# A fused DiT block on one core: 2 MB pieces for the last expert weights, transposes in place of matmuls, loads and evictions moved

## The chip, the cores and the metric

One core of one Trainium2 chip runs the whole block. The metric is device time in microseconds (us); the kernel before took 1190.56 us, the median of three runs (1188.13 to 1192.37). All data are float32 unless named otherwise.

## The reference, cut to what matters

A DiT block over 256 tokens of width 1024 with 256 context tokens: modulation vectors from a condition, an input projection, two attention branches of 8 heads each (global, and a window with a sink), gates, an output projection, a router, and 32 experts of which each token uses 4; then a final RMS norm.

```python
h = modulate(rms_norm(x, norm1_g[l]), sh1, sc1)
p = h @ w_in[l]                                   # k, v, q and two gates
y_a = global_attn(q_a, ...); y_b = window_attn(q_b, ..., sink[l])
x = x + g1 * merge_branches(y_a, y_b, g_a, g_b, w_br_a[l], w_br_b[l], w_o[l])
h2 = modulate(rms_norm(x, norm2_g[l]), sh2, sc2)
...
top_logit, top_idx = lax.top_k(t @ w_router + b_router, TOP_K)
for e in range(N_EXPERTS):
    u = t @ w_e1[e] + b_e1[e]                     # 1024 -> 2048
    act = u_glu * sigmoid(SWIGLU_ALPHA * u_glu) * (u_lin + 1)
    out = out + combine[:, e:e + 1] * (act @ w_e2[e] + b_e2[e])
x = x + g2 * out
return rms_norm(x, final_g)
```

Almost all bytes are expert weights: 32 times 8 MB for the first matrix and 4 MB for the second.

## The kernel before, in words

**Weights.** The list `pieces` (lines 45 to 86) names every weight transfer in the order in which it is used; `pump` (line 99) issues them on SP's queue in that order, each into a free part of a ring: four tiles of 8192 columns (4 MB each, `ring`), and later `xxp` (8192 columns, given at line 638) and `r_qt` (4096 columns, given at line 820). `done` (line 141) gives a part back when the matmuls that read it have been written in the program, and calls `pump`; on the chip the issue waits on SP until those matmuls have run. An expert's first matrix is four quarters of 2 MB (two of the eight k-blocks each), its second two halves of 2 MB; experts below `N_ONE = 10` are fetched in these 2 MB pieces. From expert 10 on two neighbouring pieces are one transfer of 4 MB. Expert 31's first matrix is three pieces of 2 MB and two of 1 MB, and the second matrices of experts 30 and 31 come together in column groups (`w2l`): three pieces of 2 MB, two of 1 MB.

**Attention.** Eight units `u` (a pair of heads each), two query halves `qt`. The loop at line 611 holds for each half: two `turn`s (line 549: four transposes of the weights P each into bank `tp`, evicted by ACT for the even and DVE for the odd one), `scores` of the next unit (line 514: two matmuls, DVE maximum over 1024 columns, two Exp on ACT), `y_steps`, once per unit `weigh` of the unit before (line 563: its result goes into the one bank `y`), half a gate projection, the reciprocal of the sums (`norm_p`) and one or two products of the modulation matrix (`mod_v` on DVE, `mod_p` and `mod_a` on POOL and ACT). `y_steps` (line 581) empties the bank `y`: ACT copies its right half (line 578), DVE multiplies (line 579). The order of these calls is the order of the instructions on each engine; nothing reorders them.

**Router.** The loop at line 749 makes the second residual; `stats` and `squares` fill the router's logits. `x1_back` (line 789) then puts the residual, transposed by matmuls with the identity (line 794), into the four accumulator banks `acc`, eight blocks of 128 by 128 for each token half; half 0 stands ahead of the top-k's counts (lines 814 to 818), half 1 behind them. ACT issues the loads of `g2` (a row broadcast to 128 partitions) and `be2` behind the loop (lines 780 and 784). `pick` (line 826) writes the selection matrix that `gather` (line 847) multiplies with.

**Experts.** For each expert e the loop at line 1002 writes: `scatter` of the pair before, bias, `gemm1` (line 881) of the next expert for the k-blocks of its first piece, with the transposes of e's activation (`act_turn`) behind the first k-block, then `gemm2` (line 929) of e, the rest of `gemm1`, and the activation. `steps` (line 982) hangs `spread` and `pick` into an even next expert and `gather` into an odd one, behind a named k-block.

**End.** Five column groups of the last pair (`last2`, line 1041), each with its `share` of the sum, squares and gain; then `total` and `finish` for each token half, and the two output transfers.

Of the kernel before, what the change touches and what calls it, by code (L numbers as in the profile page):

```python
# [18 lines left out]
N_ONE = 10  # L19
# [16 lines left out]
def tile_dit_block(ctx: ExitStack, tc: tile.TileContext, xcT, consts, small, rows,  # L36
# [16 lines left out]
    def w1s(e, ks):  # L53
        if ks in ((0, 1), (2, 3)) and e >= N_ONE:
            pieces.append(("w1", (e, ks[0]), w1[e, ks[0] // 2]))
        else:
            pieces.extend(("w1", (e, k), w1[e, k // 2, :, 4096 * (k % 2):4096 * (k % 2) + 4096]) for k in ks)

    def w2s(e):
        if e < N_ONE:  # L60
            pieces.extend(("w2", (e, k), w2[e, :, 4096 * k:4096 * k + 4096]) for k in range(2))
        else:
            pieces.append(("w2", (e, 0), w2[e]))
# [13 lines left out]
    for e in range(NE - 2):  # L77
        n = 2 if e + 1 >= N_ONE else 1
        w1s(e + 1, tuple(range(n)))
        w2s(e)  # L80
        w1s(e + 1, tuple(range(n, 4)))
# [529 lines left out]
    for u in range(8):  # L611
        for qt in range(2):
            turn(u, 2 * qt)
# [3 lines left out]
            y_steps()  # L617
# [113 lines left out]
    LOW_R, MID_R, ALL_R = slice(96, 128), slice(64, 96), slice(64, 128)  # L731
    for r in (slice(0, 32), MID_R, LOW_R):
        nc.scalar.dma_start(out=braw[r, :], in_=b1e)
# [15 lines left out]
    for m in range(8):  # L749
# [17 lines left out]
        bias_parts(m)  # L767
        if m == 1:
# [11 lines left out]
    nc.scalar.dma_start(out=g2, in_=g2_dram[0:1, :].to_broadcast([128, 1024]))  # L780

    x_t, y_t = t8[0].rearrange("p (a c) -> p a c", a=2), [t8[1].rearrange("p (a c) -> p a c", a=2)]
    be2 = y_t[0][:, 1, 0:512]
    nc.scalar.dma_start(out=be2, in_=b2)
# [4 lines left out]
    def x1_back(tb):  # L789

        for h in range(2):
            acc[tb, h] = ps2.tile([128, 512], F32, name="acc", tag=("xg", "sp")[tb], bufs=2)
            for b in range(4):
                nc.tensor.matmul(acc[tb, h][:, 128 * b:128 * b + 128], x1T[:, 4 * h + b, 128 * tb:128 * tb + 128],
                                 ident, start=(b == 0), stop=False, skip_group_check=True)
# [85 lines left out]
    def gemm1(e, u, ks, between=None):  # L881
        p, j = divmod(e, 2)
        for k in ks:
            if e == NE - 1 and k > 5:
                w = take("l1", k - 6)
            else:
                big = ("w1", (e, 2 * (k // 4) if N_ONE <= e < NE - 1 else k // 2))
                o = 2048 * (k % 4 if N_ONE <= e < NE - 1 else k % 2)
# [7 lines left out]
            elif k % (4 if N_ONE <= e < NE - 1 else 2) == (3 if N_ONE <= e < NE - 1 else 1):  # L896
# [32 lines left out]
    def gemm2(e, aT):  # L929
        p, j = divmod(e, 2)  # L930
        y = ps2.tile([128, 512], F32, name="y", tag="y")
        for k in range(8):
            n = 4 if e < N_ONE else 8
# [48 lines left out]
    def steps(e):  # L982
# [11 lines left out]
        if e == 1:  # L994
            return {3: lambda: gather(p + 1), 6: settle}
        return {3: lambda: gather(p + 1)}
# [5 lines left out]
    for e in range(NE - 2):  # L1002
# [4 lines left out]
        n = 4 if N_ONE <= e + 1 < NE - 1 else 2  # L1007
# [98 lines left out]
    square(4, 1, False)  # L1106
    finish(0)
    total(1)
# [185 lines left out]
```

## Time and profile before

| | |
|---|---|
| median of 3 runs | 1190.56 us (1188.13 to 1192.37) |
| the profiled execution's own time | 1187.26 us |
| its span | 1185.5 us |
| busy: PE (TensorE matmul) | 1108.2 us, 93% |
| busy: DVE (VectorE), ACT (ScalarE), POOL (GpSimd) | 324.8, 143.6 and 48.0 us |
| bytes moved | 458.83 MB, mean 387 GB/s |
| chain that ended last | PE 59%, DMA 34%, DVE 4%, ACT 2% |

SP only issues transfers. "Idle before" of an engine is put down to what ended it. Since matmuls overlap, a busy PE is not a PE at its peak; whether PE or the transfers bound a stretch is read from who waits for whom there.

### The profile page before, as it was taken

To read this page: it belongs to the slowest core of one execution; us is meant where nothing else is said; L and a number is where in the kernel's file an instruction comes from. 1 tells how busy PE (TensorE), PEld (TensorE's weight loads), DVE (VectorE), ACT (ScalarE), POOL (GpSimd) and SP (SyncE) were. 2 spreads that over 40 slices of the span, in tenths; PEclk is the share of its full clock that TensorE was granted. 3 is DMA by queue.
4 is the path that set the end of the run, shared out by engine and by line. 5 is a ranking of instruction groups with operands and counts; after the bars stand their busy time and mean duration, and the time that the engine had idled before them with its cause. 6 is when DMAs were issued, how large, how long until landed. Compare 5 with 4: busy or idle time off the path is not lost.

```text
span 1185.5 us, 13010 instructions
## 1 busy us (share of the span) xinstructions
PE 1108.2 (93%) x5610; PEld 528.0 (45%) x5610; DVE 324.8 (27%) x711; ACT 143.6 (12%) x313; POOL 48.0 (4%) x37
## 2 busy tenths in 40 slices
PE   7999999999999999999999998989898989898986
PEld 5888666894334334343333333333333333333224
DVE  3273666343222221221212112121212121212123
ACT  2122554031000000000000000000000000000002
POOL 0232100030000000000000000000000000000001
PEclk9999999999999999999999999999999999999998
DMA  9995643959999999999999999999999999999994
GB/s 377 380 399 206 221 141 143 392 181 398 429 427 429 427 428 428 427 434 431 427 435 430 427 435 431 431 431 427 434 432 428 434 427 434 431 430 432 427 425 177
DMA packets 28735, 458.83 MB, mean 387 GB/s; under 512 B 3609, under 2 KB 4001, under 8 KB 6049
## 3 DMA queue, kind: packets, MB, share of 16 engines
q1 hardware_dynamic: 26928, 454.05, 90.9%
q10 hardware_dynamic: 1744, 3.90, 1.0%
q8 instruction: 46, 0.75, 0.3%
q14 instruction: 17, 0.13, 0.0%
HBM read 456.88 MB, written 1.05 MB: 386 GB/s over the span
## 4 chain that ended last, share of the span: by engine, by line
PE 59%; DMA 34%; DVE 4%; ACT 2%; issue 1%; ACTq 0%; DVEq 0%
DMA ring<-w 27%; PE u L892 24%; PE y L937 8%; DMA xxp<-w 7%; PE mm L395 3%; PE xg L855 3%; PE qa L296 2%; PE acc L953 2%; PE o L753 2%; PE br L599 2%; ACT xxp L537 1%; PE yl L1047 1%; PE kp L385 1%; PE vp L469 1%; PE ta L925 1%; DVE st L527 1%
## 5 line engine op out<-in xcount | busy, mean ns | idle before, releaser
L892 PE MATMUL u<-ring,t 128*64 128x512 f32 x1552 | 354.0, 602 | 22.2 <-DMA ring<-w 22.1
L892 PEld LDWEIGHTS u<-ring,t 128*64 128x64 f32 x1552 | 108.2, 138 | 231.6 <-issue 193.7
L937 PE MATMUL y<-ring,tmp 128*64 128x512 f32 x768 | 169.9, 594 | 17.3 <-DMA ring<-w 11.0
L944 DVE TENSOR_TENSOR t<-y,r_kv 64x512 f32<-64x512 f32 x60 | 41.3, 688 | 334.2 <-PE y L937 333.6
L937 PEld LDWEIGHTS y<-ring,tmp 128*64 128x64 f32 x768 | 53.6, 137 | 120.9 <-issue 100.1
L892 PE MATMUL u<-xxp,t 128*64 128x512 f32 x416 | 96.9, 613 | 5.4 <-DMA xxp<-w 5.4
L909 ACT ACTIVATE tmp<-tmp 128x512 f32<-128x512 f32 (+1 forms) x33 | 20.3, 617 | 629.0 <-DVE tmp L908 629.0
L908 DVE TENSOR_SCALAR tmp<-u 128x512 f32<-128x512 f32 (+1 forms) x33 | 22.3, 675 | 227.8 <-PE u L892 215.9
L855 PEld LDWEIGHTS xg<-r_kv,r_y 128*128 128x128 f32 x512 | 58.4, 192 | 12.2 <-issue 12.2
L855 PE MATMUL xg<-r_kv,r_y 128*128 128x128 f32 x512 | 61.3, 278 | 0.0
L395 PE MATMUL mm<-xxp,ring 128*128 128x256 f32 x256 | 59.9, 385 | 0.0
L953 PE MATMUL acc<-t,r_kv 128*128 128x512 f32 x120 | 59.5, 618 | 0.0
L857 DVE TENSOR_TENSOR t<-xg,modb 128x512 f32<-128x512 f32 x32 | 22.1, 691 | 132.9 <-PE xg L855 132.9
L892 PEld LDWEIGHTS u<-xxp,t 128*64 128x64 f32 x416 | 29.3, 140 | 63.5 <-issue 53.0
L395 PEld LDWEIGHTS mm<-xxp,ring 128*128 128x128 f32 x256 | 47.3, 190 | 12.6 <-issue 5.0
L937 PE MATMUL y<-xxp,tmp 128*64 128x512 f32 x176 | 39.0, 594 | 4.7 <-DMA xxp<-w 3.1
L1071 POOL TENSOR_TENSOR ring<-ring 128x256 f32<-128x256 f32 (+1 forms) x8 | 5.1, 660 | 894.4 <-DMA ring<-rows 892.7
L953 PEld LDWEIGHTS acc<-t,r_kv 128*128 128x128 f32 x120 | 20.3, 189 | 38.7 <-issue 38.7
L296 PE MATMUL qa<-xxp,ring 128*128 128x256 f32 x128 | 30.7, 388 | 0.0
L926 ACT COPY tmp<-ta 128x512 f32<-128x512 f32 x30 | 17.6, 585 | 103.5 <-PE ta L925 103.5
L753 PE MATMUL o<-r_qt,ring 128*128 128x256 f32 x128 | 28.9, 380 | 0.0
L353 DVE SCALAR_TENSOR_TENSOR ring<-ring,crow 128x1024 f32<-128x1024 f32 x22 | 26.3, 1211 | 0.0
(237 smaller groups left out, 852.7 us busy)
## 6 DMA issues: line engine op xcount, KB each, us to landing
ring<-w SPq DMA_DIRECT2D x49, 4096.0 KB, 40.4
ring<-w SPq DMA_DIRECT2D x47, 2048.0 KB, 18.5
xxp<-w SPq DMA_DIRECT2D x13, 4096.0 KB, 40.7
xxp<-w SPq DMA_DIRECT2D x10, 2048.0 KB, 16.5
ring<-w_mod SPq DMA_DIRECT2D x16, 1024.0 KB, 10.7
r_qt<-w SPq DMA_DIRECT2D x6, 2048.0 KB, 21.5
ring<-w_in SPq DMA_DIRECT2D x10, 1024.0 KB, 8.5
ring<-w_m SPq DMA_DIRECT2D x8, 1024.0 KB, 12.4
```

What stands on the lines that cost most here:

```text
L296: nc.tensor.matmul(qa[c // 4][:, c % 4, :], w[:, 128 * c:128 * c + 128], x[:, j, :], start=(j == 0 and c % 2 == 0), stop=(j == 7), skip_gr ...
L353: nc.vector.scalar_tensor_tensor(out=w, in0=w, scalar=1.0, in1=crow, op0=ALU.mult, op1=ALU.mult, accum_out=moda[:, t:t + 1])
L395: nc.tensor.matmul(gp[0][:, 0:256], w[:, k, :], x[:, k, :], start=(k == 0), stop=(k == 7))
L599: nc.tensor.matmul(ps[:, 0:256], w[:, k, 128 * (m % 2):128 * (m % 2) + 128], Y[:, 4 * br + k, :], start=(k == 0), stop=(k == 3))
L753: nc.tensor.matmul(ps[:, 0:256], w[:, k, :], M[:, k, :], start=(k == 0), stop=(k == 7))
L855: nc.tensor.matmul(xp[:, b, :], z[:, tb, 128 * k:128 * k + 128], S[:, tb, :], start=(tb == 0), stop=(tb == 1))
L857: nc.vector.tensor_tensor(out=XT[p][:, 4 * h:4 * h + 4, :], in0=xp, in1=sh2[:, 4 * h:4 * h + 4].unsqueeze(2).to_broadcast([128, 4, 128]), ...
L892: nc.tensor.matmul(u[c0:c0 + 64, ch % 2, :], XT[p][:, k, 64 * j:64 * j + 64], w[:, 512 * ch:512 * ch + 512], start=(e == 0 and k == 0), st ...
L908: nc.vector.tensor_scalar(out=w(glu), in0=v[:, bs, 0, :], scalar1=LIMIT, scalar2=None, op0=ALU.min)
L937: nc.tensor.matmul(y[64 * h:64 * h + 64, :], l, w[:, 512 * h:512 * h + 512], start=(k == 0), stop=(k == 7))
L944: nc.vector.tensor_tensor(out=YY[p][64 * j:64 * j + 64, 512 * h:512 * h + 512], in0=y[64 * h:64 * h + 64, :], in1=g2[64 * h:64 * h + 64, 5 ...
L953: nc.tensor.matmul(acc[tb, h], t[:, tb, :], y[:, s], start=False, stop=False, skip_group_check=True)
```

## The change

It does six things. Experts from `N_TWO = 29` on are fetched in 2 MB pieces again (expert 29 and 30's first matrices, expert 29's second), and `gemm1` and `gemm2` follow. `y_steps` moves from behind the next unit's scores to the head of each half. The loads of `g2` and `be2` are issued in the output projection's loop at m = 2, `be2` into another tile. The residual's matmuls with the identity carry `is_transpose`. `gather` hangs behind k-block 2 in place of 3. At the end `total(1)` stands ahead of `finish(0)`.

```diff
@@ -16,7 +16,7 @@
 DRAM = bass.MemoryType.DRAM
 
 NE = 32
-N_ONE = 10
+N_ONE, N_TWO = 10, 29
 CAP = 64
 EPS = 1e-6
 ALPHA = 1.702
@@ -51,13 +51,13 @@
         pieces.extend(("mod", i, w_mod[i]) for i in ids)
 
     def w1s(e, ks):
-        if ks in ((0, 1), (2, 3)) and e >= N_ONE:
+        if ks in ((0, 1), (2, 3)) and N_ONE <= e < N_TWO:
             pieces.append(("w1", (e, ks[0]), w1[e, ks[0] // 2]))
         else:
             pieces.extend(("w1", (e, k), w1[e, k // 2, :, 4096 * (k % 2):4096 * (k % 2) + 4096]) for k in ks)
 
     def w2s(e):
-        if e < N_ONE:
+        if not N_ONE <= e < N_TWO:
             pieces.extend(("w2", (e, k), w2[e, :, 4096 * k:4096 * k + 4096]) for k in range(2))
         else:
             pieces.append(("w2", (e, 0), w2[e]))
@@ -75,7 +75,7 @@
     pieces.extend(("wo", i, w_o[i]) for i in range(4))
     w1s(0, range(4))
     for e in range(NE - 2):
-        n = 2 if e + 1 >= N_ONE else 1
+        n = 2 if N_ONE <= e + 1 < N_TWO else 1
         w1s(e + 1, tuple(range(n)))
         w2s(e)
         w1s(e + 1, tuple(range(n, 4)))
@@ -610,11 +610,12 @@
 
     for u in range(8):
         for qt in range(2):
+
+            y_steps()
             turn(u, 2 * qt)
             turn(u, 2 * qt + 1)
             if u < 7:
                 scores(u + 1, qt)
-            y_steps()
             if u and qt == 0:
                 weigh(u - 1)
             if u < 7:
@@ -729,6 +730,7 @@
     braw = t8[1]
     b1e = b1.rearrange("(e c) n -> e (c n)", c=4)
     LOW_R, MID_R, ALL_R = slice(96, 128), slice(64, 96), slice(64, 128)
+    be2 = msc[:, 1:3, :].rearrange("p a b -> p (a b)")
     for r in (slice(0, 32), MID_R, LOW_R):
         nc.scalar.dma_start(out=braw[r, :], in_=b1e)
 
@@ -765,6 +767,10 @@
             stats(*pend)
         pend = (m, zt)
         bias_parts(m)
+        if m == 2:
+            nc.scalar.dma_start(out=g2, in_=g2_dram[0:1, :].to_broadcast([128, 1024]))
+
+            nc.scalar.dma_start(out=be2, in_=b2)
         if m == 1:
 
             ws = mtx[:, 3, :].rearrange("p (k e) -> p k e", k=8)
@@ -777,11 +783,7 @@
             nc.vector.tensor_tensor(out=lb, in0=lp[:, 0:32], in1=brb, op=ALU.add)
     squares(sqs)
     stats(*pend)
-    nc.scalar.dma_start(out=g2, in_=g2_dram[0:1, :].to_broadcast([128, 1024]))
-
     x_t, y_t = t8[0].rearrange("p (a c) -> p a c", a=2), [t8[1].rearrange("p (a c) -> p a c", a=2)]
-    be2 = y_t[0][:, 1, 0:512]
-    nc.scalar.dma_start(out=be2, in_=b2)
 
     nc.scalar.activation(out=junk, in_=eps, func=AF.Exp)
     acc = {}
@@ -792,7 +794,7 @@
             acc[tb, h] = ps2.tile([128, 512], F32, name="acc", tag=("xg", "sp")[tb], bufs=2)
             for b in range(4):
                 nc.tensor.matmul(acc[tb, h][:, 128 * b:128 * b + 128], x1T[:, 4 * h + b, 128 * tb:128 * tb + 128],
-                                 ident, start=(b == 0), stop=False, skip_group_check=True)
+                                 ident, start=(b == 0), stop=False, is_transpose=True, skip_group_check=True)
 
     x1_back(0)
     nc.vector.reciprocal(rt, rt)
@@ -884,8 +886,8 @@
             if e == NE - 1 and k > 5:
                 w = take("l1", k - 6)
             else:
-                big = ("w1", (e, 2 * (k // 4) if N_ONE <= e < NE - 1 else k // 2))
-                o = 2048 * (k % 4 if N_ONE <= e < NE - 1 else k % 2)
+                big = ("w1", (e, 2 * (k // 4) if N_ONE <= e < N_TWO else k // 2))
+                o = 2048 * (k % 4 if N_ONE <= e < N_TWO else k % 2)
                 w = take(*big)[:, o:o + 2048]
             for ch in (0, 2, 1, 3):
                 c0 = 64 * (ch // 2)
@@ -893,7 +895,7 @@
                                  w[:, 512 * ch:512 * ch + 512], start=(e == 0 and k == 0), stop=(e > 0 and k == 7))
             if e == NE - 1 and k > 5:
                 done("l1", k - 6)
-            elif k % (4 if N_ONE <= e < NE - 1 else 2) == (3 if N_ONE <= e < NE - 1 else 1):
+            elif k % (4 if N_ONE <= e < N_TWO else 2) == (3 if N_ONE <= e < N_TWO else 1):
                 done(*big)
             if between and k in between:
                 between[k]()
@@ -930,7 +932,7 @@
         p, j = divmod(e, 2)
         y = ps2.tile([128, 512], F32, name="y", tag="y")
         for k in range(8):
-            n = 4 if e < N_ONE else 8
+            n = 8 if N_ONE <= e < N_TWO else 4
             w = take("w2", (e, k // n)).rearrange("p (k c) -> p k c", k=n)[:, k % n, :]
             l = aT[:, k % 4, 64 * (k // 4):64 * (k // 4) + 64]
             for h in range(2):
@@ -992,8 +994,8 @@
                 s[5] = lambda: pick(p + 1)
             return s
         if e == 1:
-            return {3: lambda: gather(p + 1), 6: settle}
-        return {3: lambda: gather(p + 1)}
+            return {2: lambda: gather(p + 1), 6: settle}
+        return {2: lambda: gather(p + 1)}
 
     u0 = ps2.tile([128, 2, 512], F32, name="u", tag="u")
     gemm1(0, u0, range(8), steps(0))
@@ -1004,7 +1006,7 @@
         if p:
             scatter(p - 1, (j,))
         u = bias1(e + 1)
-        n = 4 if N_ONE <= e + 1 < NE - 1 else 2
+        n = 4 if N_ONE <= e + 1 < N_TWO else 2
         gemm1(e + 1, u, (0,))
         aT = act_turn(e)
         gemm1(e + 1, u, range(1, n), steps(e + 1))
@@ -1104,8 +1106,8 @@
     total(0)
     square(3, 1, False)
     square(4, 1, False)
+    total(1)
     finish(0)
-    total(1)
     finish(1)
 
 
```

How the change moves instructions at three places follows, as the built programs have them. First DVE in the attention, around the second half of unit 1. L579 is the multiplication that empties bank `y`, L556 the eviction of an odd turn, L527 the maximum of the scores, L547 the reciprocal, L353 a product of the modulation matrix. Before:

```order
L353 SCALAR_TENSOR_TENSOR ring_65,moda<-ring_65,crow 128x1024
L556 COPY xxp<-tp 128x4x128
L527 TENSOR_REDUCE st<-s 128x2
L530 TENSOR_TENSOR st<-st,nrs 128x2
L579 TENSOR_TENSOR r_y<-y,r 128x256
L547 RECIPROCAL st<-st 128x2
```

DVE at the same place of the changed program:

```order
L353 SCALAR_TENSOR_TENSOR ring_65,moda<-ring_65,crow 128x1024
L579 TENSOR_TENSOR r_y<-y,r 128x256
L556 COPY xxp<-tp 128x4x128
L527 TENSOR_REDUCE st<-s 128x2
L530 TENSOR_TENSOR st<-st,nrs 128x2
L547 RECIPROCAL st<-st 128x2
```

The multiplication has moved ahead of the eviction and the maximum; on ACT the copy (L578) has moved ahead of the even eviction in the same way.

Second, SP's queue at the end, from the last 4 MB pieces to the final gains (128x8192 is 4 MB, `ring_62` to `ring_65` are the ring's tiles). Before:

```order
L135 DMA ring_65<-w 128x8192
L135 DMA ring_62<-w 128x8192
L135 DMA xxp<-w 128x8192
L135 DMA ring_63<-w 128x8192
L135 DMA ring_64<-w 128x8192
L135 DMA ring_65<-w 128x8192
L135 DMA r_qt<-w 128x4096
L135 DMA ring_62<-w 128x4096 x2
L135 DMA xxp<-w 128x2048 x2
L135 DMA xxp<-w2l 128x4096
```

SP's queue from the same weight on in the changed program:

```order
L135 DMA r_qt<-w 128x4096
L135 DMA ring_65<-w 128x8192
L135 DMA ring_62<-w 128x4096 x2
L135 DMA xxp<-w 128x4096 x2
L135 DMA ring_63<-w 128x4096 x2
L135 DMA ring_64<-w 128x4096 x2
L135 DMA r_qt<-w 128x4096
L135 DMA ring_65<-w 128x4096 x2
L135 DMA ring_62<-w 128x4096
L135 DMA ring_62<-w 128x2048 x2
L135 DMA xxp<-w2l 128x4096 x2
```

Five transfers of 4 MB have become ten of 2 MB, the first and the last of which go to `r_qt`; the bytes and the order of the weights are the same.

Third, PE where expert 30's first matrix (L892 before, L894 with the change) runs beside expert 29's second (L937, then L939); `ta` is the activation's transposes, `tq` those of the scatter matrix. Before:

```order
L892 MATMUL u<-ring_63,t_70 64x512 x4
L925 MATMUL ta<-keep,tmp_1339 128x128 x4
L892 MATMUL u<-ring_63,t_70 64x512 x12
L875 MATMUL tq<-keep,tmp_1339 128x128 x2
L937 MATMUL y<-ring_64,tmp_1339 64x512 x16
L892 MATMUL u<-ring_65,t_70 64x512 x16
```

PE at the same place of the changed program:

```order
L894 MATMUL u<-xxp,t_70 64x512 x4
L927 MATMUL ta<-keep,tmp_1339 128x128 x4
L894 MATMUL u<-xxp,t_70 64x512 x4
L939 MATMUL y<-ring_63,tmp_1339 64x512 x16
L894 MATMUL u<-ring_64,t_70 64x512 x8
L877 MATMUL tq<-keep,tmp_1339 128x128 x2
L894 MATMUL u<-ring_64,t_70 64x512 x8
L894 MATMUL u<-r_qt,t_70 64x512 x8
```

Two k-blocks stand ahead of the second matrix in place of four, and the last six come from three pieces in place of one.

## Rows read from the trace of the kernel before

**Rows 1.** The page's slices of the span: GB/s moved in each of 40.

```profile
GB/s 377 380 399 206 221 141 143 392 181 398 429 427 429 427 428 428 427 434 431 427 435 430 427 435 431 431 431 427 434 432 428 434 427 434 431 430 432 427 425 177
```

**Rows 2.** PE's waits over the span: for whom, us in total, times, longest.

```profile
PE u L892 <- DMA ring<-w: 22.1, 14, 2.7
...
PE y L937 <- DVE t L857: 7.8, 10, 0.8
...
PE y L569 <- DVE r_y L579: 4.3, 6, 1.7
```

**Rows 3.** Stretches (us): each engine's busy time, then granted clock, DMA share, GB/s.

```profile
278.00:279.00 1.00, 1.00 (x8) 0.32 (x6) 0.00 (x0) 0.00 (x0) 0.00 (x0) 1.00 0.12 49
300.00:500.00 200.00, 198.09 (x958) 75.38 (x955) 45.13 (x89) 9.99 (x18) 0.00 (x0) 1.00 1.01 428
600.00:1100.00 500.00, 457.98 (x2142) 169.88 (x2144) 96.22 (x188) 23.63 (x42) 0.00 (x0) 0.98 1.00 431
603.00:604.00 1.00, 1.00 (x4) 0.24 (x2) 0.00 (x0) 0.00 (x0) 0.00 (x0) 0.50 0.84 360
```

**Rows 4.** SP's timeline, 260 to 292 us: start, length, what is issued.

```profile
271.20 0.33 SPq L135 DMA_DIRECT2D r_qt<-w  x1
278.32 7.20 SPq L135 DMA_DIRECT2D ring<-w  x3
```

**Rows 5.** The page's DMA issues: count, KB each, median us from issue to landing.

```profile
ring<-w SPq DMA_DIRECT2D x49, 4096.0 KB, 40.4
ring<-w SPq DMA_DIRECT2D x47, 2048.0 KB, 18.5
```

**Rows 6.** Timeline of one attention unit: start, us, engine, line; brackets: idle before, releaser.

```profile
168.38 0.69 DVE L556 COPY xxp<-tp 128x512 f32<-128x512 f32 x1
...
173.49 0.69 DVE L556 COPY xxp<-tp 128x512 f32<-128x512 f32 x1
...
175.20 1.04 PE L553 MATMUL tp<-keep,xxp 128*128 128x128 f32 x8
...
177.45 0.43 DVE L579 TENSOR_TENSOR r_y<-y,r 128x256 f32<-128x256 f32 x1 [1.75 <-ACT r L578]
...
177.93 0.66 PE L569 MATMUL y<-keep,st 128*64 128x128 f32 x8 [0.42 <-DVE r_y L579]
...
179.19 0.69 DVE L556 COPY xxp<-tp 128x512 f32<-128x512 f32 x1
```

**Rows 7.** The same timeline, where the last unit begins.

```profile
199.54 0.66 PE L569 MATMUL y<-keep,st 128*64 128x128 f32 x8 [1.69 <-DVE r_y L579]
```

**Rows 8.** Timeline of the router, 266 to 272 us.

```profile
266.94 1.95 PE L794 MATMUL acc<-keep,r_qt 128*128 128x128 f32 x16
...
268.70 0.20 DVE L810 TENSOR_SCALAR mask_b<-r_kv 128x64 bf16<-128x64 f32 x1
...
269.09 2.03 PE L794 MATMUL acc<-keep,r_qt 128*128 128x128 f32 x16
...
269.59 0.98 DVE L831 TENSOR_SCALAR r_kv<-keep,rankm,rt 128x64 f32<-128x64 f32 x4
...
270.96 3.74 PE L855 MATMUL xg<-r_kv,r_y 128*128 128x128 f32 x32
```

**Rows 9.** PE's timeline, the last 70 us.

```profile
1119.13 7.09 PE L937 MATMUL y<-ring,tmp 128*64 128x512 f32 x32 [1.52 <-DMA ring<-w]
1128.89 7.09 PE L892 MATMUL u<-ring,t 128*64 128x512 f32 x32 [2.67 <-DMA ring<-w]
...
1165.03 3.67 PE L1047 MATMUL yl<-ring,t 128*64 128x256 f32 x32
```

**Rows 10.** Timeline of the last 10 us, DVE: second token half's total and reciprocal.

```profile
1178.01 0.15 DVE L1074 TENSOR_REDUCE fin<-fin 128x1 f32<-128x4 f32 x1
...
1178.71 0.16 DVE L1082 RECIPROCAL fin<-fin 128x1 f32<-128x1 f32 x1 [0.36 <-ACT fin L1077]
```

**Rows 11.** The chain that ended last: start, us, what.

```profile
601.24 8.78 PE u L892 x32
```

## The prediction

> **What bounds the kernel now.** I read the page first: its slices of GB/s [rows 1] show two stages. From the eleventh slice on (about 300 us) the rate stands at 425 to 435 in all but the last; ahead of that it rises and falls, down to 141. So from about 280 us to the end the transfers bound the time, and before it something else does. PE's list of waits [rows 2] agrees: what PE waits for most is a weight in the ring, 22.1 us under the first line alone. Next, SP's timeline [rows 4] and a fine cut [rows 3] show what starts the full-rate stage: at 278 to 279 us the transfers run at 49 GB/s, and the issue at 278.32 ends that. That issue waits for PE to have read the first piece of expert 0. All that follows goes at 428 to 431 GB/s whatever PE does. The rule for this kernel: what brings PE earlier at 278 us shifts the whole stream, and with it the end; what brings PE earlier inside the stream only makes it wait longer; and what PE still has to do behind the last weights comes on top.
>
> Ahead of 278 us PE itself is busy nearly all the time. Its only repeated wait in the attention is for bank `y`: 4.3 us in six times, the longest 1.7 [rows 2].
>
> **The attention's eviction first.** The multiplication that frees the bank stands behind the next scores' maximum and exponentials, so PE waits 0.42 us at 177.93 [rows 6] and 1.69 at the last unit [rows 7]. Moved ahead of the turns it finds its input long ready and the bank is free half a unit earlier. All 4.3 us could go: the upper bound. The lower bound is the chain on DVE and ACT. From one odd eviction to the next it takes 5.11 us in the half without the multiplication (168.38 to 173.49) and 5.70 in the half with it (to 179.19) [rows 6]. The half that loses it falls to 5.11; the half that gains it grows by the 0.35 us that DVE gives it before its next instruction. A unit then takes 10.57 in place of 10.81, 0.24 less; over the five full units 1.2 us. Which end? PE would save 2.6 us (4.3 less the 1.69 of the last unit) in these units, the chain 1.2; PE may run ahead of the chain by the time between the odd eviction's end and the transposes that reuse its bank, which start at 175.20, the odd ones 0.5 later [rows 6]: 1.5 us, less 0.35 for the later eviction. 1.2 and 1.15 make 2.35. The last unit's 1.69 goes almost whole, since that eviction now stands a full half earlier: 1.55. I take **3.9 us**, and keep 1.2 and 4.3. What waits behind the moved multiplication, the odd eviction, has that same slack; ACT's copy is covered by its idle time ahead of the exponentials.
>
> **Transposes.** Eight matmuls with the identity take 1.95 us (they run as 16 passes) [rows 8]; eight transposes of the same shape in the attention 1.04 [rows 6]. That is 0.9 for each half. [...] The first half saves nothing: PE then waits for the mask, which DVE ends at 268.90, where PE was through at 268.89 [rows 8]. Behind the second half stands `gather`, which needs the selection written from 269.59 to 270.57; it started at 270.96. So 0.4 is sure and 0.9 the most; I take **0.45**. The matmuls into the same accumulators are not shown as transposes in this trace, so that they gain nothing is the lower bound.
>
> **Early loads.** Two ACT issues and 0.75 MB leave 267 us, where the stream is busy, for some 247, in the slice that moves only 181 GB/s [rows 1]. ACT's work behind them isn't on PE's path, and the stream is idle before 278.32 anyway [rows 3]: **0**. It keeps the issue at 271.20, past which it moves, clear when all comes 4 us earlier.
>
> **`gather` one k-block earlier.** It removes 7.8 us of PE's waits (ten times 0.8 [rows 2]), all in experts where PE waits for the stream afterwards: **0**. It puts 3.8 us of matmuls [rows 8] ahead of a release; a transfer is issued 40.4 us before it lands, at 4 MB [rows 5], of which it moves for 9.7, so 30 us cover that.
>
> **2 MB pieces at the end.** Weights land 9.76 us apart for 4 MB (1119.13 to 1128.89), and PE needs 7.09 for them [rows 9]. At 1128.89 PE starts on 4 MB; with two pieces half of it is read by then, and PE is through 3.55 us earlier. From there on weights land each 4.88 us for 2 MB, 2.44 for 1 MB: 6, 2, then three column groups of 2 MB each, the last of these at 1128.89 + 7 x 4.88 = 1163.05. PE takes it up at 1165.03 [rows 9]; it can be at most **1.95** earlier, and 3.5 of lead, less some 1.2 of waiting for expert 31's third piece, suffice for that. The bounds are 0 and 2.4. Against it, 20 MB more go in 2 MB pieces, which ran at 428 GB/s where 4 MB ran at 431 [rows 3]: 49 us by 0.7%, **0.3 lost** (0 to 0.3). `r_qt`, idle before until the end, takes the first piece, so no place is missing.
>
> **The end.** The second half's total and root take 0.70 us from 1178.01 to 1178.71 [rows 10] behind the first half's scaling; now they run beside it, and cost the first half's output 0.4, which isn't last. DVE's own two short operations stay: **0.35** (0 to 0.4).
>
> **Sum.** 3.9 + 0.45 + 1.95 + 0.35 - 0.3 = 6.35, say 6.3. The profiled execution took 1187.26 us (span 1185.5): 1181.0 with the change. It stands 3.3 below the median of the three runs, 1190.56; for a median I forecast **1184.3**.
>
> **Rivals.**
> [...]
> - *DVE's chain alone sets the attention*: 1.2 in place of 3.9, 1187.0. Against it, the slack above. 0.10.
> - *The front's gain never reaches the stream*, because another wait holds the issue at 278.32: only the tail is left, 1188.6. Against it, transfers are idle just then [rows 3]. 0.10.
> - *The finer end does not do what it says*, PE having other waits there: 1186.2. 0.05.
> - *Slower: the release behind `gather`.* In nine odd experts with 4 MB pieces the release comes 3.8 us later. It decides where less than 3.8 us of issued work is left for the transfers; then up to 9 x 3.8 = 34 us are added, 1218. Against it 40.4 us [rows 5]; for it the first 2 MB pieces, 18.5 us, where cover is thin at one place. 0.03.
>
> **Numbers.** The forecast has 0.60. A measurement of this kernel can tell 0.3% from no change, 3.6 us: faster is below 1187.0. From the cases: 0.60 x 0.95 + 0.12 x 0.85 + 0.10 x 0.5 + 0.10 x 0.15 + 0.05 x 0.85 makes 0.78, with the rest of the cases 0.19 for the same, and 0.03 slower. The range: all upper bounds together give 1.6 less, and three runs spread by 2 to each side, so I start at 1181.0; the upper end takes in the stream that doesn't shift, 1188.6.
>
> **What would show it.** PE's wait for `y` at the weighing gone, and the last weighing at about 206 in place of 209.8; the issue of the first piece after expert 0's at about 274; the second `acc` group of the residual near 1 us; ten waits for the gather's eviction gone, with the waits for the ring longer by as much; no wait over 1.5 us behind the last pieces; granted clock 1.00 through the router. The prediction is wrong if the stream begins no earlier, if PE waits for odd evictions in the attention, or if the rate of the last 50 us falls under 428.

## The result, and the profile after

| | before | after |
|---|---|---|
| median of 6 runs each | 1190.75 us (1188.13 to 1192.37) | 1183.08 us (1180.77 to 1185.55) |
| the profiled execution | 1187.26 us, span 1185.5 | 1182.69 us, span 1180.9 |

The ratio of the times is 0.9945 (95% interval 0.9926 to 0.9963): 0.55% faster. The medians lie 7.7 us apart, the two profiled executions 4.6; where the other 3 us are is told with the experiments.

First the attention. The first and the last weighing in PE's timeline of the kernel before (start, length, instruction):

```profile
134.55 0.66 PE L569 MATMUL y<-keep,st 128*64 128x128 f32 x8
...
209.83 0.66 PE L569 MATMUL y<-keep,st 128*64 128x128 f32 x8
```

The same of the changed kernel, the weighings of units 0, 1, 5, 6 and 7:

```profile
134.67 0.66 PE L569 MATMUL y<-keep,st 128*64 128x128 f32 x8
144.70 0.66 PE L569 MATMUL y<-keep,st 128*64 128x128 f32 x8
...
186.36 0.66 PE L569 MATMUL y<-keep,st 128*64 128x128 f32 x8
195.63 0.66 PE L569 MATMUL y<-keep,st 128*64 128x128 f32 x8
206.28 0.66 PE L569 MATMUL y<-keep,st 128*64 128x128 f32 x8
```

None has a bracket any more: the waits for bank `y` [rows 6, 7] are gone. The first weighing starts 0.12 later than before (134.55), the last at 206.28 in place of 209.83, so from first to last it is 71.61 us where it was 75.28: **3.67 gained**.

Two small waits of PE are new. In the second halves of three units the eight transposes of the turns take 1.25 to 1.27 us in place of 1.04, because the weight load (PEld) waits for the odd eviction, which now stands behind the multiplication. And in the last unit PE waits for ACT's tanh of a gate, which empties bank `mm` (L397):

```profile
173.34 1.25 PE L553 MATMUL tp<-keep,xxp 128*128 128x128 f32 x8
...
173.94 0.42 PEld L553 LDWEIGHTS tp<-keep,xxp 128*128 128x128 f32 x4 [0.23 <-DVE xxp L556]
...
198.30 3.72 PE L599 MATMUL mm<-r_y,ring 128*128 128x256 f32 x16 [0.28 <-ACT t L397]
```

The first three distances between weighings are 10.03 to 10.32 us, the next two 10.53 and 10.56.

The router, the same instructions as in [rows 8]:

```profile
263.39 1.04 PE L796 MATMUL acc<-keep,r_qt 128*128 128x128 f32 x8
265.15 0.20 DVE L812 TENSOR_SCALAR mask_b<-r_kv 128x64 bf16<-128x64 f32 x1
265.40 0.19 PE L816 MATMUL rk<-mask_b,tri 128*128 128x32 bf16 x1 [0.98 <-DVE mask_b L812]
265.54 1.07 PE L796 MATMUL acc<-keep,r_qt 128*128 128x128 f32 x8
266.03 0.98 DVE L833 TENSOR_SCALAR r_kv<-keep,rankm,rt 128x64 f32<-128x64 f32 x4
267.21 3.81 PE L857 MATMUL xg<-r_kv,r_y 128*128 128x128 f32 x32 [0.60 <-PE acc L796]
```

Eight transposes take 1.04 and 1.07 us, where eight matmuls took 1.95 and 2.03. Most of both savings turns into PE's waits: 0.98 for the mask, as forecast, and 0.60 in front of the gather. That second bracket names PE's own residual, which had ended 0.6 before; what ended last is VectorE's selection, 266.03 + 0.98 = 267.01. The gather starts 0.20 behind it, where it was 0.39 [rows 8], and takes 3.81 us in place of 3.74. The first release of the weight stream shows what is left. SP's queue:

```profile
266.69 0.33 SPq L135 DMA_DIRECT2D r_qt<-w  x1
274.65 7.19 SPq L135 DMA_DIRECT2D ring<-w  x3
```

From the last weighing to this issue it is 68.37 us; before it was 278.32 - 209.83 = 68.49 [rows 4, 7]. So transposes, early loads and the earlier issue of the piece in `r_qt` gave **0.12** together.

PE's waits over the span (for whom, total, times, longest), the three that answer to [rows 2]:

```profile
PE u L894 <- DMA ring<-w: 25.7, 20, 2.6
PE y L939 <- DMA ring<-w: 10.6, 7, 1.5
...
PE u L894 <- DMA r_qt<-w: 1.2, 1, 1.2
```

The ten waits of 0.8 for the gather's eviction are gone, and those for the ring are longer in sum. The stream still sets the pace. Stretches of 300 to 500, 600 to 1060 and 1060 to 1160 us (busy time of each engine, granted clock, DMA share, GB/s):

```profile
300.00:500.00 200.00, 198.03 (x958) 75.46 (x957) 45.78 (x89) 10.63 (x19) 0.00 (x0) 1.00 1.01 428
600.00:1060.00 460.00, 422.23 (x1976) 155.11 (x1974) 88.56 (x170) 22.43 (x40) 0.00 (x0) 0.99 1.00 431
1060.00:1160.00 100.00, 93.78 (x458) 35.90 (x456) 20.80 (x44) 7.62 (x15) 0.00 (x0) 0.98 1.00 424
```

PE at the last weights, against [rows 9]:

```profile
1125.48 3.65 PE L894 MATMUL u<-r_qt,t 128*64 128x512 f32 x16 [1.24 <-DMA r_qt<-w]
...
1140.17 7.09 PE L894 MATMUL u<-ring,t 128*64 128x512 f32 x32 [0.97 <-DMA ring<-w]
...
1159.93 3.67 PE L1049 MATMUL yl<-ring,t 128*64 128x256 f32 x32 [0.16 <-DMA ring<-w2l]
```

Expert 30's last weights are there at 1125.48, where they were at 1128.89: 3.41 earlier, so 0.26 of the front's gain is lost on the way; that the slower pieces cost it is borne out by the run with 2 MB pieces alone, below. PE takes up the third column group 34.45 us later in place of 36.14: **1.69** gained. From there to the last copy of a sum it is 10.92 us in both. The end before (VectorE's last copy, the second output's issue; then KB and us from issue to landing):

```profile
1175.95 0.52 DVE L1058 COPY ring<-acc 128x128 f32<-128x128 f32 x2 [0.36 <-PE acc L1057]
...
1179.82 0.35 ACTq L1088 DMA_DIRECT2D out<-ring  x1
```
```profile
out<-ring ACTq DMA_DIRECT2D x1, 512.0 KB, 3.8
```

The end of the changed kernel (with both issues):

```profile
1170.85 0.52 DVE L1060 COPY ring<-acc 128x128 f32<-128x128 f32 x2 [0.36 <-PE acc L1059]
...
1173.31 0.34 SPq L1090 DMA_DIRECT2D out<-ring  x1
...
1174.18 0.35 ACTq L1090 DMA_DIRECT2D out<-ring  x1
```
```profile
out<-ring SPq DMA_DIRECT2D x1, 512.0 KB, 3.1
out<-ring ACTq DMA_DIRECT2D x1, 512.0 KB, 5.3
```

From that copy to the last issue it is 3.33 us in place of 3.87 (1175.95 to 1179.82): 0.54 gained. But the two outputs are issued 0.87 apart, not 1.58, and the second lands 5.3 us after its issue, where before it took 3.8. From the last issue to the end of the execution's time it is 8.51 us, against 7.44: 1.07 given back.

The profiled executions add up: -0.12 + 3.67 + 0.12 - 0.26 + 1.69 + 0.54 - 1.07 = 4.57. The first term (the start, which the change doesn't touch) and the last (the landing) differ from one execution to the next; the five between them make 5.76.

### The profile page after: what moved, and what is told of

It reads as the page before. It is cut to its first block, busy times and chain, and to the rows that moved or that the text cites. A ratio compares the mean times of both kernels' runs of the same rounds, so it can differ in the third digit from the quotient of the medians.

```text
span 1180.9 us, 12994 instructions
## 1 busy us (share of the span) xinstructions
PE 1107.9 (94%) x5594; PEld 526.3 (45%) x5594; DVE 326.5 (28%) x711; ACT 143.4 (12%) x313; POOL 47.4 (4%) x37
## 4 chain that ended last, share of the span: by engine, by line
PE 61%; DMA 36%; DVE 1%; issue 1%; ACT 1%; ACTq 0%; SPq 0%; DVEq 0%
DMA ring<-w 23%; PE u L894 21%; PE y L939 9%; DMA xxp<-w 6%; PE xg L857 5%; PE mm L395 5%; DMA r_qt<-w 3%; DMA ring<-w2l 3%; PE qa L296 2%; PE o L755 2%; PE acc L955 2%; PE br L599 2%; PE s L519 1%; PE kp L385 1%; PE vp L469 1%; PE tp L553 1%
## 5 line engine op out<-in xcount | busy, mean ns | idle before, releaser
L894 PE MATMUL u<-ring,t 128*64 128x512 f32 x1552 | 357.7, 605 | 25.8 <-DMA ring<-w 25.7
L894 PEld LDWEIGHTS u<-ring,t 128*64 128x64 f32 x1552 | 107.2, 139 | 234.8 <-issue 186.9
L939 PE MATMUL y<-ring,tmp 128*64 128x512 f32 x768 | 169.4, 593 | 10.6 <-DMA ring<-w 10.6
L939 PEld LDWEIGHTS y<-ring,tmp 128*64 128x64 f32 x768 | 54.4, 137 | 117.5 <-issue 105.3
L894 PE MATMUL u<-xxp,t 128*64 128x512 f32 x400 | 92.6, 606 | 6.4 <-DMA xxp<-w 6.2
L894 PEld LDWEIGHTS u<-xxp,t 128*64 128x64 f32 x400 | 27.6, 138 | 59.3 <-issue 48.0
L939 PE MATMUL y<-xxp,tmp 128*64 128x512 f32 x176 | 38.9, 593 | 3.0 <-DMA xxp<-w 3.0
L353 DVE SCALAR_TENSOR_TENSOR ring<-ring,crow 128x1024 f32<-128x1024 f32 x22 | 26.3, 1211 | 0.0
```

What stands on the lines that cost most here:

```text
L353: nc.vector.scalar_tensor_tensor(out=w, in0=w, scalar=1.0, in1=crow, op0=ALU.mult, op1=ALU.mult, accum_out=moda[:, t:t + 1])
L894: nc.tensor.matmul(u[c0:c0 + 64, ch % 2, :], XT[p][:, k, 64 * j:64 * j + 64], w[:, 512 * ch:512 * ch + 512], start=(e == 0 and k == 0), st ...
L939: nc.tensor.matmul(y[64 * h:64 * h + 64, :], l, w[:, 512 * h:512 * h + 512], start=(k == 0), stop=(k == 7))
```

## Experiments

The theory, from here on T: the time is start + attention + router + a stream of fixed length + what stands behind its last weights; each edit is worth what it does to its own summand. Rivals stand with each run. The first four ran on one chip beside the kernel before (1188.49 us, median of 23 runs), the next four on another (1190.24, 15 runs), the last four on a third (1191.46, 11 runs). So only ratios or traces are compared across the chips.

**The attention alone, and all but the attention.** In the kernel before `y_steps` goes to the head of the half; in the changed one it goes back.

```diff
+            y_steps()
             turn(u, 2 * qt)
             turn(u, 2 * qt + 1)
             if u < 7:
                 scores(u + 1, qt)
-            y_steps()
```

> The kernel before with only the eviction of bank y moved to the head of each half. My theory (PE ran ahead of the DVE chain, and the front's gain passes to the stream one to one): the last weighing starts near 206.3 us in place of 209.8, the issue behind expert 0's first piece near 274.8 in place of 278.3, and the run is 3.5 us shorter than before (3 to 4). Rival (the DVE and ACT chain alone sets the pace): last weighing near 208.3, 1.2 to 1.7 us shorter. Rival (the stream does not follow the front): the weighing moves, the time stays within 1 us.

> The change without the attention's move. My theory: the last weighing is back at 209.8 us with six waits for bank y, 4.3 us in all; the issue behind expert 0's first piece at 278.1, 0.2 earlier than before; the time is 3.5 us over the changed kernel's and 2 to 4 under the kernel before. Rival (most of the gain lies in the finer pieces at the end): within 1.5 us of the changed kernel.

Alone: 1184.92 us, ratio 0.9970 (0.9957 to 0.9982). Undone: 1186.15, ratio 0.9980 (0.9967 to 0.9992). First to last weighing 71.57 and 75.29 us. So the attention is worth 3.6 to 3.7 in the weighings and 3.57 in the medians, and the rest of the change about 2.3 in the medians: 5.9 in all on this chip, near the 5.76 of the steps. Release behind last weighing: 68.48 and 68.37, the same 0.11 for the transposes. But the profiled execution of the attention alone took 1188.17 us, longer than the kernel before's own. Stretches show why (16 to 19, 21 to 24, 1127.4 to 1136 us):

```profile
16.00:19.00 3.00, 2.07 (x18) 1.79 (x17) 1.71 (x5) 1.17 (x2) 1.65 (x2) 1.00 1.02 415
21.00:24.00 3.00, 3.00 (x15) 2.45 (x12) 0.87 (x3) 0.37 (x1) 0.00 (x0) 0.71 1.05 427
...
1127.40:1136.00 8.60, 8.58 (x32) 2.59 (x32) 0.00 (x0) 0.00 (x0) 0.00 (x0) 0.80 0.99 423
```

Twice the granted clock falls from the 1.00 of the first stretch: to 0.71 and to 0.80. Near 20 us, after waits of 0.68 and 0.25, it moves the first weighing to 136.83, 2.3 later than before. At 1127.42, after a wait of 2.64 us for expert 30's last 4 MB, 32 matmuls take 8.78 us in place of 7.09:

```profile
1127.42 8.78 PE L892 MATMUL u<-ring,t 128*64 128x512 f32 x32 [2.64 <-DMA ring<-w]
```

The kernel before's profiled execution has neither at these two places.

**The pieces undone.** The changed kernel with 4 MB pieces up to expert 30 (expert 31 was finer in both).

```diff
-N_ONE, N_TWO = 10, 29
+N_ONE, N_TWO = 10, 31
```

> The change with the last experts' weights in 4 MB pieces as before. My theory: PE reaches the third column group of the last pair 1.7 us later against the landing of expert 30's last weights (36.1 us behind it in place of 34.4), so 1.7 us over the changed kernel. Rival (2 MB pieces lower the stream's rate and eat it): no difference, the landing of expert 30's last weights 0.3 us or more earlier than in the changed kernel and the tail longer by as much. Rival (most of the median's gain over the profile's is a clock drop in the tail that finer pieces avoid): 3 us or more over, with granted clock under 1 behind 1080 us.

1184.02 us, ratio 0.9959 (0.9944 to 0.9974); the profiled execution took 1188.37 and again has the fall at the start (first weighing 136.64) and in the tail:

```profile
1128.92 8.55 PE L894 MATMUL u<-ring,t 128*64 128x512 f32 x32 [2.64 <-DMA ring<-w]
```

From the first release to the last output's issue: 902.47 us here, 899.53 in the changed kernel, 901.50 in the kernel before, which has the old end order (0.54) and no fall. The pieces without a fall are thus worth 901.50 - 899.53 - 0.54 = 1.43 net, and with it 2.94: the theory's 1.7 (less the rate's 0.26) and the last rival's 3 both occur, in different executions. A third loss shows here, the only other one in front of the release (timeline, 237 to 245 us):

```profile
239.67 2.05 POOL L740 CAST be<-t 32x2048 bf16<-32x2048 f32 x1 [26.32 <-DMA t<-b]
239.89 2.11 DVE L777 TENSOR_TENSOR t<-r_kv,modb 128x256 f32<-128x256 f32 x1
242.04 2.59 DVE L779 TENSOR_TENSOR t<-t 128x128 f32<-128x128 f32 x3
242.12 2.20 POOL L747 TENSOR_TENSOR t<-t,be 64x1024 f32<-64x1024 f32 x1 [0.40 <-ACT be L745]
...
244.68 0.41 PE L782 MATMUL lp<-t,ones 128*128 128x32 f32 x2 [1.45 <-DVE t L779]
```

VectorE's multiplication took 2.11 us, as long as GpSimd's cast beside it lasted (0.42 where it began no later than the cast), and the additions behind it 2.59 beside GpSimd's next instruction (0.78 in the changed kernel's first profile). PE waited 1.45, and the release came 70.09 us after the last weighing.

**The end undone.**

```diff
-    total(1)
     finish(0)
+    total(1)
     finish(1)
```

> The change with the second half's total behind the first half's finish again. My theory: the last output's issue comes 0.4 to 0.5 us later behind the last eviction of the accumulator (3.9 us in place of 3.3), and the time is within 0.5 us of the changed kernel's. Rival (two outputs issued 0.9 us apart in place of 1.6 land later by what was won, 5.3 us in place of 3.8 from issue): the last landing comes at the same distance from the last eviction, so nothing is won.

1182.76 us, ratio 0.9949 (0.9935 to 0.9962), where the changed kernel has 0.9945. Its end:

```profile
1171.16 0.52 DVE L1060 COPY ring<-acc 128x128 f32<-128x128 f32 x2 [0.36 <-PE acc L1059]
...
1173.45 0.34 SPq L1090 DMA_DIRECT2D out<-ring  x1
1175.04 0.35 ACTq L1090 DMA_DIRECT2D out<-ring  x1
```

3.88 us from copy to issue against 3.33: the 0.55 at the issue is real. What it is worth in time is blurred by the landing of the second output. With the new order that took 4.0 to 5.3 us in eleven profiles, with the old one 3.8 to 4.5 in three; from copy to the end of the time that makes 10.5 to 11.8 and 11.3 to 12.0, on average 11.1 and 11.6. The two ranges overlap, so the gain is shown at the issue; in time 0.5 is only the likeliest value, and the rival (nothing won) is not ruled out.

**The transposes undone.** The residual's blocks are turned by plain matmuls again.

```diff
-                                 ident, start=(b == 0), stop=False, is_transpose=True, skip_group_check=True)
+                                 ident, start=(b == 0), stop=False, skip_group_check=True)
```

> The changed kernel with its residual transposes as plain matmuls again. Theory (the faster transposes hardly help, because the gather waits for the router's pick on VectorE, not for the residual): a pass of eight takes 1.95 us instead of 1.04, the router's matmuls for both token blocks come some 0.9 us later each, VectorE's pick still ends within 0.2 us of where it does in the changed kernel relative to the last attention weighing, and the time is 0 to 0.3 us longer. What changes is only when PE reaches the gather. Rival (the prediction's own term): the gather and with it the last release come 0.45 us later, the median is 0.45 us longer. Rival 2: both passes are on the path, +1.8 us.

1181.74 us, ratio 0.9935 (0.9920 to 0.9950): not slower. The release stands 68.49 us behind the last weighing, 0.12 more than with transposes. In the trace the first expectation holds, and 0.45 and 1.8 are out; 0.12 us in the time is less than six runs can tell, and the changed kernel did not run beside this one. The distance is that of the kernel before (68.49), so the early loads, which no run undoes by themselves, are worth nothing in it.

**The gather back.**

```diff
-        return {2: lambda: gather(p + 1)}
+        return {3: lambda: gather(p + 1)}
```

> The changed kernel with the gather of the next pair one step later again (after gemm step 3). Theory (the weights bound that stretch): some ten waits of 0.8 us of PE for VectorE's copy of the gathered tokens come back, 7 to 8 us in all; the waits for weights shrink by as much (25.7 to about 22 us), and the time is the same within 0.3 us. Rival (PE's lost time reaches the end): slower by up to 7 us.

1183.83 us, ratio 0.9951 (0.9933 to 0.9969). PE's list of waits:

```profile
PE u L894 <- DMA ring<-w: 22.2, 19, 2.8
...
PE y L939 <- DVE t L859: 7.1, 9, 0.8
```

The gather's waits are back and the ring's shorter; from the release to the last issue it is 899.56 us against 899.53. The gather's place is worth nothing, as T has it. In front of the release this execution lost time twice: the 1.45 of the cast, and this in the router (the second pass; stretches of 260 to 266.4 and 266.4 to 268.4 us):

```profile
266.46 1.95 PE L796 MATMUL acc<-keep,r_qt 128*128 128x128 f32 x8
```
```profile
260.00:266.40 6.40, 5.41 (x42) 4.83 (x41) 2.45 (x15) 3.27 (x8) 0.48 (x2) 0.97 0.63 223
266.40:268.40 2.00, 2.00 (x14) 1.91 (x15) 1.64 (x8) 1.89 (x4) 0.00 (x0) 0.50 1.01 434
```

The granted clock is 0.50, right behind the wait of 0.98 for the mask. The transposes take 1.95 in place of 1.07, and so use up the wait in front of the gather; the gather, still in part at the lower clock (0.87 from 268.4 to 272.5 us), takes 4.37 in place of 3.81:

```profile
268.20 4.37 PE L857 MATMUL xg<-r_kv,r_y 128*128 128x128 f32 x32
```

The release comes 70.72 us behind the last weighing. Where only the cast got in the way it came 70.1 behind (three profiles, 70.08 to 70.16), so this fall cost 0.6. The next run shows both losses too (70.58 us, the gather 4.34), so there the fall cost 0.5.

**All expert weights in 2 MB pieces.**

```diff
-N_ONE, N_TWO = 10, 29
+N_ONE, N_TWO = 10, 10
```

> The changed kernel with every expert's weights in 2 MB pieces (no 4 MB pieces at all). Theory (rate): the stretch from 300 to 1060 us flows at about 428 GB/s instead of 431, so some 0.7% of 760 us: 4 to 5 us slower, and the last landing is later by as much. Rival 1 (the rate of the last stretch was low for another reason): same rate, same time within 0.5 us. Rival 2 (clock): the long waits of TensorE for 4 MB pieces become short ones, the granted clock of the stretch rises from 0.97 to 1.00, but as the weights bound it, that alone changes nothing in the time.

1186.17 us, ratio 0.9970 (0.9958 to 0.9982). The stretch:

```profile
600.00:1060.00 460.00, 416.51 (x1962) 151.44 (x1960) 87.65 (x166) 22.09 (x39) 0.00 (x0) 1.00 1.01 428
```

The rate is 428, not 431, and from the release to the last issue it is 903.90 us, 4.37 more: the rate's price, as expected. The granted clock is 1.00 (PE's longest wait for a piece in the ring is 1.3 us, where it was 2.6), and PE is busy 416.5 us where it was 422.2, with no gain. For each of the 19 experts from 10 to 28 the finer pieces cost 0.23 us; so the 20 MB of experts 29 and 30 cost about 0.4 (an estimate from this run), and 2 MB pieces pay only where PE's last work hangs on them.

**The last unit alone.**

```diff
+            if u > 5:
+                y_steps()
             turn(u, 2 * qt)
...
+            if u < 6:
+                y_steps()
             if u and qt == 0:
```

> The changed kernel with a unit's result leaving its bank at the old place for units 0 to 5 and at the new one for the last units only. Theory (each unit's wait of PE for the bank is worth its own 0.4 to 0.7 us, and the last one 1.2 to 1.7 us): from the first to the last weighing 73.3 to 73.7 us, between the 75.29 of the old place and the 71.61 of the new one; the granted clock does not matter here. Rival (the first units' waits are absorbed by VectorE's chain anyway, and only the last wait counts): 71.6 to 72.2. Rival 2 (the last one counts nothing): 75.0 to 75.3.

PE's first and last weighing (one execution):

```profile
134.12 0.66 PE L569 MATMUL y<-keep,st 128*64 128x128 f32 x8
...
207.67 0.66 PE L569 MATMUL y<-keep,st 128*64 128x128 f32 x8
```

First to last weighing 73.55 us, in place of 75.28 and 71.61. The last wait is worth 1.73 of the 3.67, the five before it 1.94 together. Both parts of the sum are there.

**Three losses that come and go.** Edits against two of them: `fill(n)` writes n matmuls of 128x128 into an unread part of a bank, in PE's waits at the start; the cast goes from GpSimd to ScalarE, three steps later (with the transposes' edit of above).

```diff
     crow_half(0)
+    fill(4)
     crow_half(1)
+    fill(1)
...
             m0_turn(k // 2)
+            if k == 0:
+                fill(2)
...
         if m == 0:
-            nc.gpsimd.tensor_copy(be1[0:32, :], braw[0:32, :])
+            return
+        if m == 3:
+            nc.scalar.copy(out=be1[0:32, :], in_=braw[0:32, :])
```

> The changed kernel as it is, once more, beside the three that follow. Theory (three small losses come and go from one execution to the next: TensorE at half its granted clock near 20 us, at half in the second pass of transposes in the router, and VectorE slowed beside the cast on GpSimd near 240 us; 2.0, about 2 and 1.45 us each): its times spread over some 4 to 5 us with the median near 1183, and its profile shows any of the three or none. Rival (the spread is the rate of the transfers): the stretch from 600 to 1060 us moves at another rate than 431 GB/s in the slower ones.

> The changed kernel with seven matmuls of 128x128 into an unread part of a bank, put into TensorE's short waits between 16 and 19 us. Theory (the waits there let the clock fall): the granted clock stays 1.00 from 0 to 25 us in this profile, the median is 0.5 to 1 us below the changed kernel's, since the fall was seen in 2 of 8 profiles so far and costs 2 us. Rival (the fall has another cause): it comes as often, and the matmuls themselves cost 0 to 0.5 us.

> The changed kernel with the residual transposes as plain matmuls again, and the cast of the first biases from GpSimd to ScalarE, three steps later. Theory (both are losses that come and go): no granted clock under 1.00 from 260 to 276 us, no wait of TensorE over 0.3 us for VectorE near 244 us, last release 68.3 to 68.5 us behind the last weighing, and a median 1.0 to 2.0 us below the changed kernel's. Rival 1 (the transposes are as good as the matmuls, their fall of the clock was chance): the same median as with the cast alone, 0.5 us below. Rival 2 (the cast on ScalarE holds up its squares): slower by up to 1 us.

> All three edits: the matmuls in the waits at the start, the plain matmuls instead of the transposes, the cast on ScalarE. Theory: the times lie closer together (within 2 to 3 us) and the median is 1.5 to 2.5 us below the changed kernel's, near 1180.5 to 1181.5, faster than both kernels. Rival: no better than the better of its two parts.

| | median (lowest to highest) | ratio to before |
|---|---|---|
| the changed kernel again | 1181.83 (1180.77 to 1183.56) | 0.9931 (0.9912 to 0.9949) |
| start filled | 1181.87 (1181.45 to 1183.97) | 0.9929 (0.9911 to 0.9946) |
| matmuls, cast on ScalarE | 1181.60 (1181.31 to 1184.03) | 0.9928 (0.9909 to 0.9946) |
| all three | 1182.61 (1181.82 to 1182.72) | 0.9933 (0.9915 to 0.9950) |

None is faster than the changed kernel: the expected 0.5 to 2.5 us are a miss, and so is the changed kernel's expected spread of 4 to 5 us: it is 2.8. With all three the six times lie within 0.9 us where the others spread over 2.5 to 2.8, so in six runs it took away spread and no median. The rival on the rate is out: the stretch from 600 to 1060 us moves at 431 GB/s in every profile but that of the run with 2 MB pieces alone. Neither filled profile has the fall near 20 us, but it is in only two of the twelve others, so whether the fill prevents it is not shown. What the fill costs isn't either: first weighings at 135.40 and 134.79, where the unfilled profiles without the fall have 133.82 to 135.00. In the two profiles with the cast on ScalarE PE does not wait at 240 us, and the release is 68.48 behind the last weighing; the start-filled one had the cast in its way (1.53, 70.16). The profile of the changed kernel run again had none of the losses, at 1180.77 us:

```profile
273.98 0.33 SPq L135 DMA_DIRECT2D ring<-w  x1
```
```profile
out<-ring ACTq DMA_DIRECT2D x1, 512.0 KB, 4.0
```

Beside the kernel before's profiled execution, 1187.26, that is 6.49 us: start 0.48, attention 3.74, router 0.12, slower stream -0.32, tail 1.68, end 0.54, and 0.25 behind the last issue. Without the start and the landing it is 5.76 again.

## Why the prediction was right

It said 1184.3 us (1181.0 to 1188.6), faster with 0.78; the median was 1183.08. Its likeliest case is the one that came. Its sum of 6.3 us was made for like executions; two executions without any of these losses lie 6.49 apart, but 0.73 of that is start and landing, and the steps themselves make 5.76. So the nearness of 6.3 and 6.49 is in part luck, and so is that of the median, which had 7.7 to fall and started from a median with losses in it (last point).

| step | forecast | measured |
|---|---|---|
| attention's eviction | 3.9 | 3.67 and 3.74 (3.57 in medians) |
| transposes | 0.45 | 0.12 |
| early loads, gather | 0 | 0 in the traces |
| 2 MB pieces | 1.95 | 1.69 and 1.68 |
| the slower rate | -0.3 | -0.26 and -0.32 |
| the end's order | 0.35 | 0.54 at the issue; in time some 0.5, not clear of the landing |

- *Attention.* The price lies between the chain's 1.2 and PE's waits, as the sum had it. The part for five units was forecast at 2.35 (1.2 of the chain and 1.15 of slack) and the last one's at 1.55; the run with the last unit alone gives 1.94 and 1.73. PE runs ahead of the chain for three units and then goes at its pace: 10.53 and 10.56 us a unit, where the forecast had the chain at 10.57. PE's waits of 0.2 for the odd evictions are that chain. The prediction's list of signs counts such a wait as being wrong, which its own sum does not bear out. What the sum lacks is the wait of 0.28 in the last unit for ACT's tanh; it is absent where only the last unit moves, and is likely most of the 0.4 by which the five units came out too high.
- *Transposes* is the step that was mis-sized. "0.4 is sure" took the gather to stand 0.4 behind the selection because of PE. In the changed kernel it starts 0.20 behind the selection's end even with PE idle for 0.60, and takes 0.07 longer; the selection itself comes no earlier (60.73 us behind the last weighing, before 60.74), since VectorE's chain makes it. The 0.9 that each pass saves is real and worth 0.12.
- *Pieces.* 7 pieces of 2 MB were to take 4.88 us each; the 34.45 us between make it 4.92. That is 0.29 over the seven, enough for the difference of 0.26. Another sign of being wrong, a rate under 428 in the last 50 us, was badly chosen: from 1110 to 1160 us the kernel before had 424 already, and the changed one has 422.
- *Rivals.* The front's gain did reach the stream (the release 3.67 earlier, the landings 3.41), the finer end did what it says, and nowhere did the gather hold up a release: 899.53 and 899.56 us. The 0.12 in the sum of chances is for a fall of the clock in the router. No run shows that number; what the runs showed is the fall in two of nine profiles with transposes (the second eight at 1.95 us in place of 1.07, the granted clock 0.50 in the one above), and in none of five with plain matmuls. Whether it lies with the transposes is not settled, since seven profiles with them have no fall, and plain matmuls also fill PE's wait of 0.98 for the mask. In both profiles with the fall the cast had got in PE's way too, so the two may hang together; that was not tried. It cost 0.6 and 0.5 us, less than the 1.7 by which 32 matmuls in the stream grew (8.78 us [rows 11] in place of 7.09 [rows 9]), since the second pass's loss fell into PE's wait of 0.60 in front of the gather.
- *The median.* What the forecast missed is that the median of before holds a loss that its profile doesn't have. Of three profiles with 4 MB pieces at the end two show the fall of the clock behind the wait of 2.64 us, 1.5 to 1.7 us each; of eleven with 2 MB pieces, where PE's waits for a piece are 1.34 at most, none does. So the pieces are worth 1.4 us in an execution without the fall and some 3 in one with it. The same fall comes all through the stream, and there no cost shows, since PE waits less for the next pieces: in the kernel before's profile 0.83 us for weights between the 8.78 at 601.24 and the next wait of 2.62, but 2.23 between the 7.09 at 718.89 and the next wait of 2.62. The changed kernel's own profile has one behind its last long wait, for expert 28:

```profile
1066.82 8.57 PE L894 MATMUL u<-ring,t 128*64 128x512 f32 x32 [2.63 <-DMA ring<-w]
```

In the run again these 32 took 7.09, and from release to last issue the two are 899.53 and 899.60. Of ten waits over 2 us for a 4 MB piece the fall follows five in the kernel before's profile and five in the changed one's. So the finer end is likely to spare about every second execution 1.5 to 1.7 us (an estimate from these counts). That goes some way to explain the 7.7, but not all: on the last chip the medians lie 9.6 apart, and there the kernel before's median is 4.7 above its own fastest run. No profile of the kernel before in such an execution was taken, so the rest stays open.

## What to carry to other kernels

Find the one issue that starts the stage that transfers bound, and price each edit by what it does to that issue or behind the last landing; all else (the gather's 7.8 us of waits, 0.9 us of faster transposes in front of another engine's result) is worth little or nothing. Finer pieces belong only to the last landings, since here they cost rate everywhere else (428 GB/s in place of 431). And where differences of 3 us matter, one profiled execution isn't the median: look in it for short stretches of lower clock (0.50 over 2 us in the router) and for instructions of several times their length (2.11 us in place of 0.42) before taking its time for typical.

## What the runs showed of the hardware

- Behind some waits for a weight the granted clock fell, even late in the kernel: 32 matmuls took 8.78 and 8.55 us in place of 7.09 behind waits of 2.64 us, with a granted clock of 0.80 in the stretch of the 8.78. A like wait of 2.67 in the kernel before's profile was followed by 7.09. In that profile and the changed kernel's first such groups took 8.57 to 8.78 us behind five of ten waits of more than 2 us each. From 600 to 1060 us the granted clock was 0.98 or 0.99 in the thirteen profiles with 4 MB pieces, and 1.00 with 2 MB pieces alone, where PE's waits for a piece were 1.3 at most. Near 20 us it fell in two of fourteen profiles (0.93 from 0 to 25 us, 1.00 in the twelve others), after waits of under 0.7.
- VectorE beside GpSimd: a multiplication of 128x256 with two inputs took 2.11 us beside GpSimd's cast of 2.05, against 0.42 where the cast ran on ScalarE. Why it is slow there is not shown. In two other profiles it was an addition of 128x256, 1.95 and 2.05 us in place of 0.43. PE waited 1.34 to 1.53 us in five of twelve profiles with that cast on GpSimd, those in which the three additions beside GpSimd's next instruction took 2.58 to 2.74 us, and in the three of them without a fall of the clock in the router the release came 70.08 to 70.16 behind the last weighing, in place of 68.37. In the changed kernel's first profile the additions took 0.78 and the multiplication alone was slow (2.11), and PE did not wait.
- Two outputs of 512 KB issued 0.65 to 1.08 us apart (eleven profiles): the second took 4.0 to 5.3 us to land, the first 3.1 to 3.4. Why it takes either was not tried.
